# Routing stage of a two-layer encoder kernel: the last tile's rows of x are stored from ACT's DMA queue instead of SP's

## The chip, the cores and the metric

The kernel runs on one core of one Trainium2 chip. The metric is the device time of the whole program in microseconds (us), the median of several executions. The profile shown below is of one execution of the same kernel.

## What is computed

Two layers work on x, 512 rows of 1024 values in float32. Each layer has a token mixer of three parts (latent attention, a matrix LSTM and a state-space scan), an output projection, a layer norm, and then a mixture of 16 experts of which every row uses two. The part of the reference around the change is this:

```
heads = jnp.concatenate([y_a, y_b, y_c], -1)
mix = jnp.einsum('bsc,cd->bsd', heads, w_out[l])
x = _layernorm(DEEPNORM_ALPHA * x + mix, ln1_g[l], ln1_b[l])
ffn = _hier_moe(x, router_group_w[l], router_group_b[l], router_expert_w[l], router_expert_b[l],
                expert_w_gate[l], expert_w_up[l], expert_w_down[l])
x = _layernorm(DEEPNORM_ALPHA * x + ffn, ln2_g[l], ln2_b[l])
...
# _hier_moe: the best of 4 groups, the best 2 of its 4 experts, weights from two softmaxes
h = jax.nn.silu(jnp.einsum('bsd,edf->bsef', x, w_gate)) * jnp.einsum('bsd,edf->bsef', x, w_up)
h = h * combine[..., None]
return jnp.einsum('bsef,efd->bsd', h, w_down)
```

## The kernel before

The 512 rows are four tiles of 128. A layer runs through the mixer, then the routing stage (output projection, first layer norm and choice of experts), then the experts one after another, then a last stage that adds up and norms. The change is in the routing stage, which each of the two layers runs once; "layer 0" and "layer 1" name the two passes.

**Routing.** Class Tile_ holds one tile's steps and the string WSEQ their order. For a tile, f finishes the first layer norm: the left half is done by ACT and POOL or, for the last tile, all of it by DVE in two pieces (L1824 to L1826), and then a DMA of 512 KB stores the tile's 128 rows into x1d, a buffer in DRAM (L1827). keep then stores the same rows into acc, where the experts' results are added later (L1831). Both stores of all tiles are issued by SP, which also issues the loads of all weights (L277). SP's instructions stand in one queue, in order.

**Experts.** An expert handles a block of 96 rows. Expert 0's rows are picked with one-hot matmuls straight from SBUF (xz). For every other expert, index forms the row numbers on PE (matmuls of tokr with the one-hot tile ohs) and on DVE (slr, slx), and gather lets POOL issue an indirect DMA that fetches the rows from x1d (L1451). The gather of expert 1 therefore waits until all four tiles' stores into x1d have landed. Behind it POOL sets a mark (L1836), and the loads that SP issues from there on are held until the mark. When the rows of expert 1 are there, x turns them on PE (eight transposes against ident into two PSUM banks, b_74 and b_73), ACT copies the high parts (xt<-b_74, xt<-b_73) and DVE forms the low parts under the same names. up(0) is the first multiplication by the expert's weights.

**Weights of the experts.** expert_weights computes, from the logits, the weight of each row and expert on DVE and ACT, and stores it as three bf16 parts in tokw: CAST tokw, subtract (wt<-wt,tokw), CAST tokw, subtract, CAST tokw. weights then has PE multiply tokw by the one-hot tiles of experts 0, 1 and 2. On PE these twelve small matmuls stand behind the transposes of expert 1 and ahead of its up(0).

**What sets the order.** The routing and the expert stage are written once; a scheduler orders each engine's instructions from the dependencies and its own estimates of time, except for those pinned with keep_in_program_order. Each engine then runs its list in order. A change of one instruction's engine can thus move others on the same and on other engines. Tiles live in 37 reused slots; the slot of the last tile's rows z becomes free for another tile only when both its stores have been read out.

Of the kernel before, what the change touches and what calls it, by code (L numbers as in the profile page):

```python
# [20 lines left out]
NT = S // 128  # L21
# [191 lines left out]
def tile_trunk(ctx: ExitStack, tc: tile.TileContext, ins, out, dbg=None, depth=DEPTH):  # L213
    nc = tc.nc
# [7 lines left out]
    class Pinned:  # L222
# [3 lines left out]
        def __getattr__(self, k):  # L226
            f = getattr(self.e, k)

            def g(*a, **kw):
                r = f(*a, **kw)  # L230
                if pin[0] and self.n in (PINS if pin[0] is True else pin[0]):
                    tc.keep_in_program_order(r)
                return r
            return g
# [321 lines left out]
    x1d = drp.tile([S, D], F32, name="x1d")  # L556
# [4 lines left out]
    for l in range(depth):  # L561
# [820 lines left out]
        def chain(f):  # L1382
            for hd in range(HEADS):
                yield from f(hd)
# [392 lines left out]
        class Tile_:  # L1777
# [42 lines left out]
            def f(self):  # L1820
                z, n = self.z, self.ph
                if n:
                    self.cp = A.activation(z[:, 0:n], z[:, 0:n], AF.Identity, scale=self.rs)
                    G.tensor_add(z[:, 0:n], z[:, 0:n], ln1[1][:, 0:n])  # L1824
                for a, b in ((n, D),) if n else ((0, 512), (512, D)):
                    V.scalar_tensor_tensor(z[:, a:b], z[:, a:b], self.rs, ln1[1][:, a:b], op0=OP.mult, op1=OP.add)  # L1826
                self.st = nc.sync.dma_start(x1d[self.s, :], z.ap)  # L1827

            def keep(self):
                tap("x1_%d_%d" % (l, self.i), self.z.ap)  # L1830
# [435 lines left out]
```

## Time and profile before

| what | us |
|---|---|
| median of 3 runs | 1042.9 (1041.09 to 1049.63) |
| the profiled execution's own time | 1043.1 |
| its span, first to last instruction | 1041.3 |
| PE busy | 985.1 (95%) |
| DVE busy | 812.8 (78%) |
| ACT busy | 632.6 (61%) |
| POOL busy | 187.4 (18%) |
| mean granted TensorE clock | 0.985 of full speed |

Times in the rows count from the span's start. The profile's groups name a line; L230 is a helper that records almost every compute instruction, so that tiles' names tell more than lines. Names are given without buffer numbers: b is a PSUM bank, s a slot, xt a tile of split operands. SPq is SP's queue of DMA issues. In a row of the timeline the bracket tells how long the engine was idle before it and what ended that.

### The profile page before, as it was taken

Reading aid. Unit: us, or ns where it says so; the run is one execution under the profiler, and the core shown is the slowest. Engines: PE = TensorE matmul, PEld = TensorE weight load, DVE = VectorE, ACT = ScalarE, POOL = GpSimd, SP = SyncE. Lnnn points to the kernel's source line nnn. Section 1 sums busy time; section 2 is a strip of 40 time slices with the busy share of each in tenths; the row PEclk is TensorE's granted clock in tenths of the full one; section 3 lists DMA queues with packets and bytes.
Section 4 is the critical chain, followed back from the end, with each engine's and each line's share of the span. In section 5 each row is a group of like instructions: output and inputs, shape, how many; then the busy total and the mean of one; then the engine's idle time right before and its main releaser. Section 6 shows DMA issues by size and latency. Waiting matters only on the chain. (4 is left out here: it accounts for less than half of the span.)

```text
span 1041.3 us, 15398 instructions
## 1 busy us (share of the span) xinstructions
PE 985.1 (95%) x5342; PEld 733.1 (70%) x5342; DVE 812.8 (78%) x1810; ACT 632.6 (61%) x1172; POOL 187.4 (18%) x172
## 2 busy tenths in 40 slices
PE   6999999999999899999899999999999979999995
PEld 6876788666688666667598767885667866667663
DVE  8995566878549799999869956588795587999986
ACT  5565635566424588889546564466672346888874
POOL 1000002242002223223000000022320112333332
PEclk9999999999999899999999999999999998999998
DMA  8201100125837789997632111001448386999944
GB/s 313 71 23 69 61 1 1 41 65 181 296 147 272 258 289 342 337 328 233 207 143 71 41 51 41 1 1 41 142 155 325 119 303 237 319 337 326 317 123 162
DMA packets 51794, 176.76 MB, mean 170 GB/s; under 512 B 8169, under 2 KB 8681, under 8 KB 51712
## 3 DMA queue, kind: packets, MB, share of 16 engines
q1 hardware_dynamic: 45216, 160.42, 43.3%
q0 software_dynamic: 6496, 15.31, 6.2%
q8 instruction: 43, 0.70, 0.3%
q14 instruction: 39, 0.32, 0.1%
HBM read 159.61 MB, written 23.59 MB: 176 GB/s over the span
## 5 line engine op out<-in xcount | busy, mean ns | idle before, releaser
L230 PE MATMUL b<-xt,s 128*128 128x512 f32 (+3 forms) x1484 | 325.3, 366 | 11.1 <-ACT s L230 9.0
L230 PE MATMUL b<-s,s 128*128 128x512 f32 (+8 forms) x1312 | 324.1, 404 | 4.8 <-ACT s L230 2.7
L230 PEld LDWEIGHTS b<-xt,s 128*128 128x128 f32 (+2 forms) x1484 | 233.4, 183 | 77.6 <-issue 12.8
L230 DVE TENSOR_TENSOR s<-s,s 128x1024 fp32r<-128x1024 f32 (+8 forms) x252 | 226.2, 922 | 56.0 <-ACT s L230 48.8
L230 ACT ACTIVATE s<-s 128x1024 fp32r<-128x1024 f32 (+4 forms) x221 | 192.4, 904 | 98.2 <-DVE s L230 38.3
L230 PEld LDWEIGHTS b<-s,s 128*128 128x128 f32 (+3 forms) x1312 | 182.8, 171 | 85.6 <-ACT s L230 18.3
L230 ACT ACTIVATE s<-b 128x512 f32<-128x512 f32 (+8 forms) x274 | 132.0, 499 | 181.0 <-PE b L230 175.7
L230 PE MATMUL b<-s,xt 128*128 128x256 f32 (+2 forms) x944 | 205.3, 357 | 0.4 <-DVE s L230 0.4
L230 PEld LDWEIGHTS b<-s,xt 128*128 128x128 f32 (+1 forms) x944 | 147.7, 186 | 36.1 <-issue 8.7
L230 DVE TENSOR_TENSOR xt<-s,xt 128x1024 fp32r<-128x1024 f32 (+1 forms) x106 | 125.8, 1193 | 14.2 <-ACT xt L230 14.0
L230 PE MATMUL b<-ident,s 128*128 128x128 f32 (+3 forms) x736 | 107.0, 271 | 20.3 <-DMA s<-x1d,slx 13.2
L230 ACT ACTIVATE xt<-s 128x1024 fp32r<-128x1024 f32 (+1 forms) x107 | 110.7, 1043 | 21.6 <-PE b L230 12.5
L230 PEld LDWEIGHTS b<-ident,s 128*128 128x128 f32 (+3 forms) x736 | 81.7, 152 | 52.1 <-DMA s<-x1d,slx 15.4
L1604 POOL DMA_INDIRECT acc<-s,slx x28 | 58.9, 2102 | 166.2 <-ACT s L230 115.5
L230 DVE TENSOR_TENSOR s<-b,s 128x192 fp32r<-128x192 f32 (+3 forms) x108 | 58.1, 549 | 15.8 <-PE b L230 10.1
L1343 POOL TENSOR_SCALAR s<-s,sums 128x512 f32<-128x512 f32 x48 | 37.3, 780 | 155.0 <-DVE sums L230 126.3
L230 ACT ACTIVATE s<-b,mx 128x512 f32<-128x512 f32 x64 | 43.9, 692 | 19.0 <-DVE mx L230 12.8
L1451 POOL DMA_INDIRECT s<-x1d,slx x30 | 40.2, 1338 | 76.9 <-PE b L230 19.2
L230 DVE TENSOR_REDUCE mx<-b 128x1 f32<-128x512 f32 x64 | 43.4, 685 | 8.8 <-PE b L230 7.9
L230 PE MATMUL b<-xt 128*96 128x512 f32 x160 | 48.1, 408 | 0.0
L230 ACT ACTIVATE s<-b,slw 96x512 f32<-96x512 f32 (+1 forms) x60 | 38.9, 683 | 5.6 <-PE b L230 3.8
L230 ACT ACTIVATE s<-s,sb 128x128 f32<-128x128 f32 x64 | 25.6, 413 | 19.4 <-DVE s L230 19.1
(251 smaller groups left out, 857.7 us busy)
## 6 DMA issues: line engine op xcount, KB each, us to landing
s<-in_w_gu_dram SPq DMA_DIRECT2D x128, 512.0 KB, 8.9
s<-in_expert_w_down_dram SPq DMA_DIRECT2D x64, 512.0 KB, 9.3
s<-in_w_inp_dram SPq DMA_DIRECT2D x36, 512.0 KB, 5.0
s<-in_w_outp_dram SPq DMA_DIRECT2D x16, 512.0 KB, 4.7
x1d<-s SPq DMA_DIRECT2D x8, 512.0 KB, 3.1
acc<-s SPq DMA_DIRECT2D x8, 512.0 KB, 4.4
s<-acc SPq DMA_DIRECT2D x8, 512.0 KB, 6.5
s<-in_x_t_dram SPq DMA_DIRECT2D x4, 512.0 KB, 5.1
```

Source lines behind the costliest of these rows:

```text
L230: r = f(*a, **kw)
L1343: (V if hd in NORMV else G).tensor_scalar(P.ap, P.ap, sums, 0.0, op0=OP.mult, op1=OP.add)
L1451: self.ga = G.indirect_dma_start(out=self.xg[:BLK], out_offset=None, in_=x1d[0:128 * n, :], in_offset=bass.IndirectOffsetOnAxis(ap=ix[:BLK ...
L1604: G.indirect_dma_start(out=acc[:, :], out_offset=bass.IndirectOffsetOnAxis(ap=self.ix[:BLK, 0:1], axis=0), in_=yt[:BLK], in_offset=None, b ...
```

## The change

The transfer that stores the rows of the last tile (i equal to NT - 1, that is 3) into x1d is issued by ACT on ACT's queue. The other three tiles' stores into x1d and all stores into acc stay on SP.

```
-                self.st = nc.sync.dma_start(x1d[self.s, :], z.ap)
+                self.st = (nc.scalar if self.i == NT - 1 else nc.sync).dma_start(x1d[self.s, :], z.ap)
```

The scheduler's lists differ in three places that matter here. SP's list only loses the store: the load of s_382 that stood behind it now stands behind the load of s_381, and the store into acc follows.

On ACT, in the routing of layer 0 (layer 1 is alike), the store stands behind the copy of bank b_69, the first half of expert 0's rows. Before:

```order
288 L230 ACTIVATE ohs_2936<-ohf_2937 128x384
289 L230 ACTIVATE s_372_3117<-b_69 128x384
290 L230 ACTIVATE s_403_3270<-s_324_2775 128x1024
291 L230 ACTIVATE s_372_3117<-b_70 128x384
292 L230 ACT_TABLE_LOAD
293 L230 ACTIVATE ge_3154<-ge_3154 128x16
294 L230 ACTIVATE xt<-s_325_2777 128x1024
295 L230 ACTIVATE md_3164<-md_3164 128x4
```

The same place as a difference:

```order
 L230 ACTIVATE s_372_3117<-b_69 128x384
-L230 ACTIVATE s_403_3270<-s_324_2775 128x1024
+L1827 DMA x1d<-s_282_2529 128x1024
 L230 ACTIVATE s_372_3117<-b_70 128x384
 L230 ACT_TABLE_LOAD
 L230 ACTIVATE ge_3154<-ge_3154 128x16
+L230 ACTIVATE md_3164<-md_3164 128x4
+L230 ACTIVATE s_403_3270<-s_324_2775 128x1024
 L230 ACTIVATE xt<-s_325_2777 128x1024
-L230 ACTIVATE md_3164<-md_3164 128x4
```

The store takes the place of a copy of weights (s_403), which moves behind the two small exponentials ge and md.

On PE, in layer 0, between the transposes of expert 1 and its up(0): ohs_2936, ohs_2939 and ohs_3250 are the one-hot tiles of experts 0, 1 and 2. Before (each pair of rows stands four times):

```order
1134 L230 MATMUL b_74<-ident,s_370_3103 128x96 x4
1135 L230 MATMUL b_73<-ident,s_370_3103 128x96 x4
1136 L230 LDWEIGHTS ohs_2936
1137 L230 MATMUL b_75<-tokw,ohs_2936 96x3
...
1144 L230 LDWEIGHTS ohs_2939
1145 L230 MATMUL b_76<-tokw,ohs_2939 96x3
...
1152 L230 LDWEIGHTS ohs_3250
1153 L230 MATMUL b_74<-tokr,ohs_3250 96x2
```

In the changed kernel the four pairs with tokr, which write into bank b_74, stand directly behind the transposes, ahead of all pairs with tokw. In layer 1 PE's list is the same in both kernels, and has tokr first already.

On DVE, in layer 0, around the low parts of expert 1's rows (xt<-b_74 and xt<-b_73). Before:

```order
623 L230 CAST tokw<-wt_3172 128x64
624 L230 TENSOR_TENSOR wt_3172<-wt_3172,tokw 128x64
625 L230 TENSOR_TENSOR s_404_3271<-s_324_2775,s_403_3270 128x1024
626 L230 CAST tokw<-wt_3172 128x64
627 L230 TENSOR_TENSOR xt<-s_325_2777,xt 128x1024
628 L230 TENSOR_TENSOR xt<-b_74,xt 128x384
629 L230 TENSOR_TENSOR xt<-b_73,xt 128x384
630 L230 TENSOR_REDUCE slw_3242<-b_75 96x1
```

And now:

```order
622 L230 TENSOR_TENSOR xt<-s_325_2777,xt 128x1024
623 L230 CAST tokw<-wt_3172 128x64
624 L230 TENSOR_TENSOR xt<-b_74,xt 128x384
625 L230 TENSOR_TENSOR wt_3172<-wt_3172,tokw 128x64
626 L230 TENSOR_TENSOR xt<-b_73,xt 128x384
627 L230 CAST tokw<-wt_3172 128x64
628 L230 COPY slr_3257<-b_74 96x1
629 L230 TENSOR_TENSOR s_406_3290<-s_406_3290,b_71 96x256
630 L230 TENSOR_TENSOR wt_3172<-wt_3172,tokw 128x64
631 L230 SCALAR_TENSOR_TENSOR slx_3256<-slr_3257,b_74 96x1
632 L230 CAST tokw<-wt_3172 128x64
```

The last CAST of tokw stood ahead of the low parts and now stands behind them, behind the copy slr of expert 2's row numbers and behind the product s_406 of expert 0. s_404, whose slot held z, stands at row 617 now, ahead of all these. In layer 1 the last CAST stood behind the low parts before as well; the same product, a subtraction and slx have come between them.

## Rows read from the trace of the kernel before

**Rows 1.** Timeline of SP, layer 0: start us, duration us, queue, line, transfer
```profile
331.76 0.43 SPq L277 DMA_DIRECT2D s<-in_w_gu_dram  x1
334.16 0.33 SPq L1827 DMA_DIRECT2D x1d<-s  x1
334.54 0.43 SPq L277 DMA_DIRECT2D s<-in_w_gu_dram  x1
335.01 1.10 SPq L1831 DMA_DIRECT2D acc<-s  x1
```

**Rows 2.** DMA issues of Rows 1: KB each, last number us from issue to landing
```profile
x1d<-s SPq DMA_DIRECT2D x1, 512.0 KB, 5.8
...
s<-in_w_gu_dram SPq DMA_DIRECT2D x1, 512.0 KB, 6.7
...
acc<-s SPq DMA_DIRECT2D x1, 512.0 KB, 7.5
```

**Rows 3.** Line L1827, all eight stores into x1d: issue to landing
```profile
DMA to landing us min/median/max: 2.6/3.1/5.8
```

**Rows 4.** Layer 1: SP's timeline, then the two stores' time to landing
```profile
848.00 0.33 SPq L1827 DMA_DIRECT2D x1d<-s  x1
848.86 1.08 SPq L1831 DMA_DIRECT2D acc<-s  x1
...
x1d<-s SPq DMA_DIRECT2D x1, 512.0 KB, 4.6
...
acc<-s SPq DMA_DIRECT2D x1, 512.0 KB, 6.9
```

**Rows 5.** Timeline of POOL: the gather of expert 1, layers 0 and 1
```profile
341.06 1.19 POOL L1451 DMA_INDIRECT s<-x1d,slx  x1 [17.67 <-DVE more L230]
...
853.60 1.12 POOL L1451 DMA_INDIRECT s<-x1d,slx  x1 [16.64 <-DVE wgt L230]
```

**Rows 6.** Timeline of PE, layer 0: transposes of expert 1, and its up(0)
```profile
345.51 1.54 PE L230 MATMUL b<-ident,s 96*128 96x96 f32 x8 [4.30 <-DMA s<-x1d,slx]
...
348.49 2.85 PE L230 MATMUL b<-xt 128*96 128x512 f32 x6
```

**Rows 7.** Timeline of PE, layer 1: transposes, tokr, tokw, up(0)
```profile
859.80 1.54 PE L230 MATMUL b<-ident,s 96*128 96x96 f32 x8 [4.73 <-DMA s<-x1d,slx]
861.94 0.40 PE L230 MATMUL b<-tokr,ohs 128*96 128x2 bf16 x4 [0.60 <-DVE s L230]
862.71 1.04 PE L230 MATMUL b<-tokw,ohs 128*96 128x3 bf16 x12 [0.36 <-DVE slr L230]
863.61 2.85 PE L230 MATMUL b<-xt,s 128*96 128x512 f32 x6
```

**Rows 8.** Timeline of DVE, layer 0: z's last piece, then s_404
```profile
333.38 0.75 DVE L230 SCALAR_TENSOR_TENSOR s<-s,nr,s 128x512 f32<-128x512 f32 x1
...
342.59 1.23 DVE L230 TENSOR_TENSOR s<-s,s 128x1024 fp32r<-128x1024 f32 x1 [0.27 <-DMA acc<-s]
```

**Rows 9.** Timeline of DVE, layer 1: expert 0's product, subtraction, last CAST of tokw
```profile
857.40 0.40 DVE L230 TENSOR_TENSOR s<-s,b 96x256 f32<-96x256 f32 x1
...
861.80 0.22 DVE L230 TENSOR_TENSOR wt<-wt,tokw 128x64 f32<-128x64 f32 x1
...
862.41 0.25 DVE L230 CAST tokw<-wt 128x64 bf16<-128x64 f32 x1
862.50 0.15 DVE L230 COPY slr<-b 96x1 f32<-96x1 f32 x1
```

**Rows 10.** Timeline of ACT: copy of bank b_69, layers 0 and 1
```profile
334.60 0.49 ACT L230 ACTIVATE s<-b 128x384 fp32r<-128x384 f32 x1 [0.75 <-PE b L230]
...
848.45 0.49 ACT L230 ACTIVATE s<-b 128x384 fp32r<-128x384 f32 x1 [0.75 <-PE b L230]
```

**Rows 11.** Busy us by stretch: PE, PEld, DVE, ACT, POOL, then PEclk, DMA, GB/s
```profile
345.30:352.00 6.70, 6.26 (x33) 5.06 (x34) 2.33 (x9) 0.98 (x2) 0.97 (x1) 0.50 0.51 194
...
857.30:867.40 10.10, 6.64 (x33) 5.27 (x34) 2.99 (x14) 0.98 (x2) 0.99 (x1) 0.50 0.50 170
```

**Rows 12.** The same view: the expert stage of layers 0 and 1
```profile
345.50:497.00 151.50, 148.25 (x768) 104.51 (x768) 137.21 (x210) 125.09 (x183) 45.66 (x28) 0.98 0.89 297
...
860.00:1010.00 150.00, 146.98 (x762) 102.46 (x762) 134.89 (x207) 121.83 (x177) 51.05 (x28) 0.98 0.85 283
```

## The prediction

> **What bounds the kernel now.** I read first the busy shares of the page: PE is busy 95% of the span, so a stall of PE is what can be won or lost. Next the table of stretches for the two expert stages: PE works 148.25 of 151.50 us and 146.98 of 150.00 us there [rows 12], so a delay at the start of this stage has almost no later gap of PE in which it could vanish, and I let it pass to the end in full. Then the timeline of PE at the start of the stage: it stands idle 4.30 us in layer 0 and 4.73 us in layer 1 until the gathered rows of expert 1 arrive [rows 6, 7]. These two stalls are the place of the change. The timelines of SP and POOL and the DMA issues show what ends them. The store of the last tile's rows into x1d is issued at 334.16 and lands after 5.8 us, at 340.0 [rows 1, 2]; the gather starts at 341.06 [rows 5], and PE at 345.51. In layer 1 the store goes out at 848.00, lands 4.6 us later at 852.6 [rows 4], the gather starts at 853.60 and PE at 859.80 [rows 5, 7]. In both layers the gather starts 1.0 to 1.1 us behind that landing. The releaser that its row names (DVE) is only the nearest update in time; the gather reads x1d and must wait for the store, and the same distance in both layers says that it does. So every us by which the store lands earlier or later moves the stall's end.
>
> **What the change removes.** It takes the store out of SP's queue. SP did not hold it up at its issue: DVE finishes the rows at 333.38 + 0.75 = 334.13 [rows 8] and SP issues at 334.16. What costs there comes after the issue. A store into x1d takes 2.6 us at best [rows 3]; this one takes 5.8 and 4.6, for the loads issued before it are still running. The transfers that follow it on SP land at 334.54 + 6.7 = 341.2 and 335.01 + 7.5 = 342.5 [rows 1, 2], so the queue delivers one transfer of 512 KB each 1.25 us or so, in the order of issue.
>
> **What it adds: a later issue on ACT.** The store now stands behind ACT's copy of b_69, which ends at 334.60 + 0.49 = 335.1 in layer 0 and at 848.45 + 0.49 = 848.9 in layer 1 [rows 10]. That is 0.9 us later than SP's issue in both. ACT's issue itself I take as SP's 0.33; it lies ahead of the copy of b_70, which waits for PE anyway, and ACT has nothing on PE's path until the rows arrive. If that cover were gone it would cost its 0.33.
>
> **How long the store then takes** is not in the trace: no transfer of the kernel before is issued by ACT. Bound below: as if alone, 2.6 us, landing at 337.7 and 851.5. Bound above: the store shares the engines so that it ends with the last of the three transfers that are under way, when acc's store ends today, 342.5 and 848.86 + 6.9 = 855.8 [rows 2, 4]. I take a value between: its own queue lets it start at once, and beside each of its packets one of SP's queue is served, so it takes the lone 2.6 plus one transfer's 1.3: 3.9 us. It then lands at 339.0 in layer 0, **1.0 us earlier**, and at 852.8 in layer 1, **0.2 us later**. The value stands nearer to the lone store because that is a row of the same transfer, and the upper bound presumes that it is served last.
>
> **Trace against page.** The rows of this case show one queue in order of issue [rows 1, 2]. The Trainium skill, page "DMA: Bandwidth & Descriptors", section "Queues, rings and completion order", says that each DMA engine takes turns packet by packet between the queues that have work; by it the sum is mine. No run here shows it for ACT.
>
> **What moves on PE and DVE.** This is the part that the diff does not tell. In layer 0 PE now has the tokr matmuls right behind the transposes. They write into b_74, which DVE must first have read for the low part. Layer 1 already has that order, so its rows price it: from the first transpose to up(0) it takes 863.61 - 859.80 = 3.81 us [rows 7], against 348.49 - 345.51 = 2.98 in layer 0 [rows 6]. Layer 0 loses **0.8 us**.
>
> In both layers DVE's last CAST of tokw, for which the twelve tokw matmuls wait, now comes behind expert 0's product, a subtraction and slx. In layer 1 before, it started at 862.41 and the tokw matmuls at 862.71 [rows 7, 9], with slr beside it at 862.50. Now slr comes first, at 862.50, then the product (0.40), the subtraction (0.22) and slx (about slr's 0.15), and then the CAST: 862.50 + 0.77 = 863.2 at small overlaps, 0.8 later than 862.41. up(0) stands behind these matmuls on PE. That is **0.8 us in each layer**, 1.6 in all. Bounds: nothing, if DVE runs ahead more than I see, and 2.4 for the three terms together as taken; I see no row for more. What hid the three instructions before was the wait for the gather: the product ran at 857.40 [rows 9], within PE's stall. That cover is gone because they now stand behind the gathered rows.
>
> **A new wait.** s_404's slot held z, so it waits for both stores. Before it started at 342.59, with acc's landing [rows 8]. DVE now has it ahead of the low parts. Behind it stand 1.23 us for itself, another weight's low part of the same size, and four small ones of 0.2: done near 345.8. The low part of b_74 is wanted about when the transposes are done, 1.54 us behind their start [rows 6], at 346.0 if the rows come 1.0 us earlier. So it is just hidden. It also caps the gain: a store that lands over 1.2 us earlier in layer 0 gives nothing more unless acc's store lands earlier too.
>
> **The sum.** -1.0 (landing, layer 0) + 0.2 (landing, layer 1) + 0.8 (PE's order, layer 0) + 1.6 (DVE's order, both) = +1.6 us. The profiled execution took 1043.1 us, 0.2 above the median of the runs, so 1044.7 us.
>
> **Rivals.**
> One, faster: the store is nearly alone on its queue (2.6 us) and the moved instructions cost nothing. Gain 1.2 (capped) and 852.6 - 851.5 = 1.1: 1043.1 - 2.3 = 1040.8. For it: half of the eight stores needed no more than the median, 3.1 [rows 3]. Against it: these were issued into an idler queue, and the DVE order is in the program.
>
> Two, slower: a second queue buys nothing, since the same engines move the bytes. Place: the store's landing. If it still takes 5.8 and 4.6 us, but starts 0.9 later in each layer, the landing terms are +0.9 and +0.9 in place of -1.0 and +0.2: 1043.1 + 1.8 + 2.4 = 1047.3. At its worst it ends with acc's store, +2.5 and +3.2: 1043.1 + 5.7 + 2.4 = 1051.2. It decides from a duration of about 4.9 us in layer 0, where the later issue eats the gain. For it: DMA is the busier the nearer the store comes. Against it: the lone store's 2.6. The Trainium skill, in the same page's section "Issuing engines are not separate DMA queues", says that starting DMAs from several engines saves only the time to issue them; it speaks for this rival, and no run here has tried it.
>
> Three, the clock. The granted clock is at half (1.2 GHz) from 345.30 to 352.00 and from 857.30 to 867.40, with PE busy 6.26 and 6.64 us in these [rows 11], after the two stalls. If a shorter stall in layer 0 keeps the clock at full (2.4 GHz), half of 6.26 comes back: 1044.7 - 3.1 = 1041.6. If the added gaps keep layer 0 at half for as long as layer 1, 3.4 us more, it loses half of that: 1046.4. For it: both stalls were followed by the fall. Against the gain: a stall of 3.3 us is left.
>
> That the change does nothing is out: the store is on ACT's list and off SP's.
>
> **Chances.** The forecast 0.50 (its own range 1043 to 1046.5); rival one 0.15; rival two 0.22, of which 0.06 lies beyond 1051; rival three 0.13, most of it the gain. The range of 1040.0 to 1050.0 takes in all but the far end of rival two. About 1% is what a measurement of this kernel can tell from no change, 10.4 us. Both stalls together are 9.0 us, so a gain over 1% would need them and the half clock gone: 0.02. A loss over 1% needs rival two beyond its worst, or more waits in the expert stage: 0.05. Within 1%: 0.93.
>
> **What would show it.** In the changed profile: the issue on ACT near 335.1 and 848.9; its time to landing near 3.9, where 2.6 is rival one and 4.6 or more is rival two; the gather about 1.0 us behind the landing; PE from first transpose to up(0) near 4.6 us in both layers, with waits for DVE ahead of the tokr and tokw matmuls; the length of the half clock. The prediction is wrong if the gather does not follow the store's landing, if DVE reaches the last CAST before the rows arrive, or if later gaps of PE in the expert stage grow or shrink by more than these terms.

## The result, and the profile after

The changed kernel takes 1051.2 us (median of 9 runs), the kernel before 1043.5 in the same number of runs beside it. The ratio is 1.006, with a 95% interval of 1.0036 to 1.0083: slower by some 6 us, less than 1%. (The two medians alone are 7.7 us apart. Below, differences of time between kernels are taken from such ratios, each to the kernel before measured beside it.) The profiled execution took 1051.1 us, its span is 1049.4 us against 1041.3 before.

The issues first: the timelines of SP and ACT in layer 0 and, behind the dots, in layer 1 (start us, duration us, queue, line, transfer, count).

```profile
331.79 1.84 SPq L277 DMA_DIRECT2D s<-in_w_gu_dram  x2
334.18 0.33 SPq L1831 DMA_DIRECT2D acc<-s  x1
...
334.69 0.34 ACTq L1827 DMA_DIRECT2D x1d<-s  x1
...
850.38 0.91 SPq L277 DMA_DIRECT2D s<-in_w_gu_dram  x2
852.78 0.33 SPq L1831 DMA_DIRECT2D acc<-s  x1
...
853.29 0.33 ACTq L1827 DMA_DIRECT2D x1d<-s  x1
```

The reader is to compare the order with [rows 1]. The store was the second of four transfers there; s_382's load and acc's store came behind it. Now SP, which no longer waits for z with the load, issues both loads in one row, then acc's store, and the x1d store is the last of the four.

POOL's gather of expert 1's rows, layers 0 and 1, answers to [rows 5]:

```profile
343.24 1.19 POOL L1451 DMA_INDIRECT s<-x1d,slx  x1 [19.82 <-DMA acc<-s]
...
862.47 1.05 POOL L1451 DMA_INDIRECT s<-x1d,slx  x1 [20.45 <-DVE tokw L230]
```

It starts 2.18 us later in layer 0. Layer 1 begins late as a whole, so there I count from the end of z's rows on DVE. z's last piece before in layer 1, then now in layers 0 and 1:

```profile
847.23 0.74 DVE L230 SCALAR_TENSOR_TENSOR s<-s,nr,s 128x512 f32<-128x512 f32 x1
...
333.41 0.74 DVE L230 SCALAR_TENSOR_TENSOR s<-s,nr,s 128x512 f32<-128x512 f32 x1
...
852.01 0.74 DVE L230 SCALAR_TENSOR_TENSOR s<-s,nr,s 128x512 f32<-128x512 f32 x1
```

Layer 1: 847.97 to 853.60 before, 5.63 us; 852.75 to 862.47 now, 9.72 us, 4.1 us more. (In layer 0 the same count is 6.93 and 9.09.)

PE, from expert 1's transposes to its up(0), in layer 0 and layer 1, answers to [rows 6, 7]:

```profile
347.82 1.54 PE L230 MATMUL b<-ident,s 96*128 96x96 f32 x8 [6.60 <-DMA s<-x1d,slx]
349.89 0.41 PE L230 MATMUL b<-tokr,ohs 128*96 128x2 bf16 x4 [0.53 <-DVE xt L230]
351.45 1.05 PE L230 MATMUL b<-tokw,ohs 128*96 128x3 bf16 x12 [1.15 <-DVE tokw L230]
...
867.13 1.54 PE L230 MATMUL b<-ident,s 96*128 96x96 f32 x8 [7.28 <-DMA s<-x1d,slx]
869.27 0.41 PE L230 MATMUL b<-tokr,ohs 128*96 128x2 bf16 x4 [0.60 <-DVE s L230]
870.80 1.05 PE L230 MATMUL b<-tokw,ohs 128*96 128x3 bf16 x12 [1.12 <-DVE tokw L230]
```

up(0) starts at 352.36 and 871.71. The way from the first transpose to it is 4.54 us where it was 2.98, and 4.58 where it was 3.81.

Last, the DMA engines from 332 to 345 us: busy tenths in 40 slices of 0.325 us, then the packets, MB and share of SP's queue (q1) and ACT's (q10).

```profile
DMA  9978887995479744779989999999999752110000
...
q1 hardware_dynamic: 811, 2.93, 64.8%
q10 hardware_dynamic: 144, 0.52, 9.9%
```

q10 is the store and nothing else. Its first packet is recorded at 338.7, 4.0 us behind the issue at 334.69 (in layer 1 it is 3.6 us; the expectation of the first run below has 338.5 and 3.8). In between the engines are down to 4 or 5 tenths twice (slices 9 and 10, 14 and 15, counted from 0), so they were not full all the time that the store waited.

### The profile page after: what moved, and what is told of

Same layout as the page of the kernel before. It is cut to its first block, busy times and chain, and to the rows that moved or that the text cites. A ratio compares the mean times of both kernels' runs of the same rounds, so it can differ in the third digit from the quotient of the medians.

```text
span 1049.4 us, 15399 instructions
## 1 busy us (share of the span) xinstructions
PE 985.1 (94%) x5342; PEld 731.9 (70%) x5342; DVE 812.9 (77%) x1810; ACT 632.5 (60%) x1172; POOL 189.6 (18%) x172
## 5 line engine op out<-in xcount | busy, mean ns | idle before, releaser
L1604 POOL DMA_INDIRECT acc<-s,slx x28 | 61.2, 2185 | 163.0 <-ACT s L230 151.5
L230 ACT ACTIVATE xt<-b 128x384 fp32r<-128x384 f32 (+1 forms) x56 | 26.9, 526 | 18.6 <-PE b L230 18.3
```

The source lines that it names most:

```text
L1604: G.indirect_dma_start(out=acc[:, :], out_offset=bass.IndirectOffsetOnAxis(ap=self.ix[:BLK, 0:1], axis=0), in_=yt[:BLK], in_offset=None, b ...
```

## The experiments

Two theories of the late landing went in. A, order of issue: what SP and ACT have issued is worked off in the order of issue, whichever queue it came by, and the store lost two places. B: a transfer on ACT's queue starts late by itself. Beside them stood the prediction's claim that the order on DVE and PE is a cost of its own.

**All four tiles' x1d stores on ACT.**

```diff
-                self.st = nc.sync.dma_start(x1d[self.s, :], z.ap)
+                self.st = nc.scalar.dma_start(x1d[self.s, :], z.ap)
```

> The stores of all four tiles' rows into x1d are issued by ACT, not the last tile's alone. Two theories of why the last tile's store landed 2.2 us later in layer 0 than before. Theory A (order of issue): the DMA engines work off what SP and ACT have issued in the order of issue, whichever queue it came by; the store lost the two places that it had ahead of s_382's load and acc's store. Theory B (late start): a transfer of ACT's queue starts about 3.8 us after its issue whatever else is under way, as the first packets did in the changed kernel (issue 334.69, packets from 338.5). The first three tiles' stores have fewer transfers ahead of them. By A they start and land as the SP stores of these tiles did, 2.6 to 3.1 us after the issue; by B their first packets come 3.8 us after the issue and they land after 5 us or more. The last tile's store is as in the changed kernel by both: gather at 343.2 in layer 0. Time: 1051 (1048 to 1054) by both, as the first tiles' stores have time.

1051.3 us, ratio 1.0071 (1.0035 to 1.0107). The last tile's gather starts 8.36 us behind z in layer 0 and 8.13 in layer 1; s_381's load moves up on SP here, so one transfer fewer is issued just ahead of the store than in the changed kernel. Tile 0's two stores are issued at the same time, with nothing else under way: the timelines of ACT and SP, then the DMA engines from 312 to 318 us (slices of 0.15 us), and the packets, MB and share of the two queues from 314.5 to 316.5 us.

```profile
313.33 0.36 ACTq L1827 DMA_DIRECT2D x1d<-s  x1
...
313.33 0.33 SPq L1831 DMA_DIRECT2D acc<-s  x1
...
DMA  0000000000000089999999999999999600000000
...
q10 hardware_dynamic: 100, 0.41, 50.9%
q1 hardware_dynamic: 96, 0.39, 48.5%
```

The engines start in slice 14, at 314.1, 0.8 us behind the issue; the first packet of ACT's queue comes at 314.5. B is out: nothing on ACT's queue waits 4 us of itself. But A's 2.6 to 3.1 us was wrong as well. Both stores run side by side and end together near 316.8, 3.5 us behind the issue; one queue would have served the x1d store first. Here the Trainium skill's rule, page "DMA: Bandwidth & Descriptors", section "Queues, rings and completion order", that each engine takes turns between queues, agrees with the trace (50.9% against 48.5% in the middle of the two stores).

**Last tile's x1d and acc stores both on ACT.** On the changed kernel:

```diff
-                hold(nc.sync.dma_start(acc[self.s, :], self.z.ap))
+                hold((nc.scalar if self.i == NT - 1 else nc.sync).dma_start(acc[self.s, :], self.z.ap))
```

> The last tile's store into x1d and its store into acc are both issued by ACT, in this order. Theory A (order of issue): acc's store now comes behind the x1d store, so the x1d store gets one of its two lost places back, 1.25 us: gather in layer 0 at 342.0 (changed kernel 343.24, before 341.06), and 1.2 us sooner after the store's issue in layer 1. Theory B (ACT's queue starts late by itself): no change, gather at 343.2. Time by A 1049 to 1050, by B 1051.

1049.1 us, ratio 1.0038 (1.002 to 1.0056), in A's range. The gather starts 7.94 us behind z in layer 0, 1.15 less than in the changed kernel; in layer 1 it is 9.42, only 0.3 less, where A had 1.2. The scheduler's order differs here too: the way from the first transpose to up(0) is 4.33 and 5.45 us, where the changed kernel has 4.54 and 4.58, so that the time is not that of the place alone.

**Only acc's store on ACT, x1d on SP.** The same edit of acc's store, on the kernel before.

> The other way round: the last tile's rows go into x1d by SP, as before, and its store into acc is issued by ACT. PE's order of layer 0 is the changed kernel's (tokr behind the transposes), and DVE's last CASTs of tokw also stand behind the low parts, so this run has the order's cost without the late store. Theories A and B both have the x1d store where it was: gather at 341.1 in layer 0 and 5.6 us behind the store's issue in layer 1, and a time of before plus the order terms (0.8 for PE in layer 0 and 0.8 for DVE in each layer), 1044.5 to 1046. A third theory, that the order of PE and DVE and not the landing made the loss, has 1049 to 1051 here. acc's store lands at 342.5 by A (it keeps its place) and at about 343 by B; s_404 waits for it.

1045.8 us, ratio 1.0015 (0.999 to 1.004). Without the late store the loss is about 1.6 us, not 6; the third theory is out. But the order is not quite the changed kernel's: the way to up(0) is 4.05 and 4.04 us, 0.5 less in each layer than there. The gather starts sooner than A had it, 339.7, but its rows came 7.2 us later, where the kernel before needed 4.45.

**One load fewer ahead, on the changed kernel.**

```diff
-NU = 7
+NU = 6
```

> The changed kernel with one load fewer issued ahead of the stage (NU 6 in place of 7): s_382's load comes behind acc's store, when the gather is already issued. Theory A (order of issue): one transfer fewer ahead of the x1d store, 1.25 us: gather in layer 0 at 342.0 and 1.2 us sooner behind the issue in layer 1; time 1049 to 1050. Theory B (late start of ACT's queue): first packets still 3.8 us after the issue, gather at 343.2 or a little sooner because fewer loads share the engines; time 1050 to 1052. If the later load of s_382 makes the expert stage wait, it shows as a wait of ACT for that load 40 us later and adds to the time by both.

1048.4 us, ratio 1.0046 (1.002 to 1.0072). The gather starts 7.70 and 8.71 us behind z, 1.4 and 1.0 less than in the changed kernel: A's 1.25. q10's first packets come 2.0 and 2.1 us behind the issue where they took 4.0 and 3.6, which B forbids.

**DVE's order taken back, on the changed kernel.**

```diff
-                V.tensor_copy(tokw[:, :, :, c], wt)
+                cast = V.tensor_copy(tokw[:, :, :, c], wt)
...
-            ex[1].x()
+            with tc.issue_after(cast.ins):
+                ex[1].x()
```

(expert_weights hands cast on.) The low parts of expert 1's rows then stand behind the last CAST.

> The changed kernel, with its store on ACT, but the two low parts of expert 1's rows queued on DVE behind the last CAST of tokw, in both layers; PE's list then has tokw, tokr, tokw behind the transposes, as layer 0 of the kernel before. The landing stays late by all theories (gather 343.2 in layer 0). If the order of DVE and PE is a cost of its own, the way from the first transpose to up(0) falls from 4.54 and 4.58 us to about 3.0 in both layers and the time by 1.5 + 1.6, to 1048. If the order only fills time in which PE would wait for something else, the way shrinks by less, or the time stays at 1051.

1047.2 us, ratio 1.0034 (1.0015 to 1.0053), 2.7 us less than the changed kernel by the ratios; the two intervals overlap, so the size rests on the rows. PE in layer 0, then the stores that SP and ACT issue at 334.59 and 335.10 (last number: us from issue to landing):

```profile
349.34 1.54 PE L230 MATMUL b<-ident,s 96*128 96x96 f32 x8 [7.70 <-DMA s<-x1d,slx]
350.68 0.77 PE L230 MATMUL b<-tokw,ohs 128*96 128x3 bf16 x8
351.42 0.41 PE L230 MATMUL b<-tokr,ohs 128*96 128x2 bf16 x4
352.05 0.41 PE L230 MATMUL b<-tokw,ohs 128*96 128x3 bf16 x4 [0.23 <-DVE slw L230]
...
acc<-s SPq DMA_DIRECT2D x1, 512.0 KB, 9.2
...
x1d<-s ACTq DMA_DIRECT2D x1, 512.0 KB, 8.2
```

The waits of 0.53 and 1.15 are gone, up(0) starts at 352.32, 2.98 us behind the first transpose, and so in layer 1. The stall ahead of it stays, 7.70 us. Order and landing are two separate costs. The gather starts at 344.36, 1.08 us behind the store's landing at 343.28. acc's store, issued 0.5 us ahead of it, lands at 343.75, behind it; in layer 1 acc's lands first, at 859.65 against 860.04. So what stands ahead on SP delays the start of the store on ACT (its first packets come 3.6 and 3.8 us behind the issue), but does not have to end ahead of it.

**The same order in the kernel before.** The last diff, on the kernel before.

> The same order of DVE's instructions in the kernel before: stores on SP, the two low parts behind the last CAST of tokw. Layer 0 had this order already (2.98 us from the first transpose to up(0)); layer 1 had 3.81. If the order is a cost of its own, layer 1 falls to about 3.0 and the time by 0.8, to 0.999 of before; else no change. The gather stays where it was, 341.1 and 853.6, by all theories.

1044.2 us, ratio 1.0007 (0.9985 to 1.0028): the 0.8 us expected can't be seen in the time, though the way in layer 1 fell from 3.81 to 2.98. In its profile the rows of layer 1 took 7.7 us behind the gather's start, 1.5 more than before. That alone would hide it; whether it does so in other executions is open.

**acc's store on ACT, with the order taken back.** The diffs of the third and the fifth run, on the kernel before.

> The x1d store on SP, acc's store on ACT and the two low parts behind the last CAST. Against the run with acc's store on ACT alone (4.05 and 4.04 us from the first transpose to up(0)) the way falls to 3.0 in both layers if the order is a cost of its own: 2.1 us less, 0.9995 of before; if not, 1.0015 of before as there. Gather at 339.7 in layer 0 and rows 7.2 us behind it, as there.

1044.6 us, ratio 0.9994 (0.9973 to 1.0014), 2.2 us below the run with acc's store on ACT alone (2.1 expected). The way is 2.98 us in both layers. In layer 0 the gather starts at 341.0 and the rows come 4.5 us later, as in the kernel before: the 339.7 and 7.2 of that other run were one execution's.

**Nothing on ACT, acc's store ahead of x1d.** On the kernel before (keep leaves acc's store out for this tile):

```diff
+                if self.i == NT - 1:
+                    hold(nc.sync.dma_start(acc[self.s, :], z.ap))
                 self.st = nc.sync.dma_start(x1d[self.s, :], z.ap)
```

> Everything on SP, nothing on ACT, but for the last tile acc's store is issued ahead of the x1d store; s_382's load comes behind both. Theory A (order of issue): the x1d store loses one place, as to acc's store in the changed kernel, without a second queue: the gather starts about 1.25 us later than before, 342.3 in layer 0 and 6.9 us behind the x1d issue of before in layer 1. A theory in which a second queue as such is what cost the 2.2 us has the gather at 341.1 to 341.5 (0.4 for the later issue). Time: before + 1.25 in each layer by A, 1046; before + 0.8 otherwise.

1047.2 us, ratio 1.0032 (1.0014 to 1.0049): slower than before without any second queue, as A has it. The profile does not show it well. The gather starts 6.63 us behind z in layer 0, earlier than A's 8.2, and 7.81 in layer 1, later than A's 6.9. That execution took 1042.2, the lowest of ten, so I don't read its layer 0 against A or for it.

**The changed kernel's order of issue, all on SP.** This is the run that tells place from queue, on the kernel before:

```diff
...
             tiles[NT - 1].keep()
+            tc.add_manual_dep(tiles[NT - 1].st.ins, tiles[NT - 1].ac.ins.name,
+                              mybir.DependencyInfo(mybir.DependencyClass.NoSync, mybir.DependencyReason.DATA))
```

(ac is acc's store; the lines that name it are left out.) SP then issues the loads of s_381 and s_382, acc's store, the x1d store.

> Everything on SP, nothing on ACT, in the order of issue of the changed kernel: the loads of s_381 and s_382, acc's store, and the x1d store last of the four. Place against queue: in the changed kernel the gather starts 9.1 us behind the end of z's rows in layer 0 (343.24 - 334.13). If the lost places alone made the store late (theory A), the gather starts 8.5 to 9.2 us behind z here too, and rows and PE follow as late as there. If ACT's queue itself adds to it, the store comes sooner here: 7.0 to 8.0 us behind z. PE's list has tokw ahead of the transposes, so the way to up(0) is about 2.3 to 3.0 us; time by A 1.003 to 1.005 of before, by the other 1.000 to 1.002.

POOL's gather in both layers, then the issues of layer 0 and of layer 1 (last number: us from issue to landing):

```profile
343.44 1.30 POOL L1451 DMA_INDIRECT s<-x1d,slx  x1 [20.18 <-issue]
...
859.62 1.11 POOL L1451 DMA_INDIRECT s<-x1d,slx  x1 [20.20 <-DVE tokw L230]
...
acc<-s SPq DMA_DIRECT2D x1, 512.0 KB, 7.1
x1d<-s SPq DMA_DIRECT2D x1, 512.0 KB, 8.0
...
acc<-s SPq DMA_DIRECT2D x1, 512.0 KB, 6.9
x1d<-s SPq DMA_DIRECT2D x1, 512.0 KB, 7.8
```

z ends at 333.99 and 850.44, so the gather starts 9.45 and 9.18 us behind it, as late as with ACT (9.09, 9.72); in layer 0 that is 0.25 past the upper end of what A expected. The landing needs no second queue to be late. The time, 1046.7 us, ratio 1.0013 (0.999 to 1.0035), is lower than A's 1.003 to 1.005 and can't be told from no change. Against the run with ACT's late store and the same way of 2.98 us (1.0034) the intervals overlap widely. Whether ACT's queue has a cost of its own that these rows don't show stays open: some 2 us by the two ratios, anything from nothing to 5 within their intervals.

**Both stores on ACT, one load fewer, order taken back.** The diffs of the second, fourth and fifth run together. The store has its place of the kernel before, on ACT's queue.

> ACT issues the last tile's x1d store and acc's store, one load fewer is issued ahead (s_382's comes later), and the two low parts stand behind the last CAST. Of what is issued before the x1d store only s_381's load is still under way: the place of the kernel before, but on ACT's queue. Theory A (place alone): gather 6.9 us behind the end of z's rows or 6.4 behind the issue, as before, time 0.999 to 1.000 of before. If ACT's queue itself adds 1 us or so: gather 7.4 us or more behind the issue in both layers, time 1.001 to 1.003.

The issues of layers 0 and 1:

```profile
x1d<-s ACTq DMA_DIRECT2D x1, 512.0 KB, 4.4
acc<-s ACTq DMA_DIRECT2D x1, 512.0 KB, 4.6
...
x1d<-s ACTq DMA_DIRECT2D x1, 512.0 KB, 5.4
acc<-s ACTq DMA_DIRECT2D x1, 512.0 KB, 5.6
```

4.4 and 5.4 us to landing, against 5.8 and 4.6 on SP [rows 2, 4]; the gather is 5.5 and 6.5 us behind the issue. 1042.4 us, ratio 0.9988 (0.9964 to 1.0012). The first packets come 1.0 and 0.8 us behind the issue, where they took 2.0 to 2.8 with one place lost (three runs) and 3.6 to 4.0 with two. In its old place the store can't be told to be slower on ACT, or faster.

**The kernel before with two loads fewer ahead, order taken back.** Both stores on SP; the fifth run's diff and

```diff
-NU = 7
+NU = 5
```

> Stores on SP as in the kernel before, the low parts behind the last CAST, and two loads fewer issued ahead of the stage: s_381's and s_382's come behind acc's store and the gather. If transfers are worked off in the order of issue, the x1d store now has nothing ahead of it but the end of older loads and lands as the earlier tiles' stores, about 3 us after its issue; the gather starts near 338.5 in layer 0, 2.5 us sooner than before, and as much in layer 1. Time by this 1038 to 1040 if the later loads make no new wait in the expert stage; 1043 or more if they do (waits of ACT or DVE for s_381 and s_382 some 30 us later) or if the gather takes longer beside them by as much as it starts sooner.

1040.8 us, ratio 0.9971 (0.9943 to 0.9998): just below the kernel before, a little above the 1038 to 1040 expected. Issues of layers 0 and 1, POOL in layers 0 and 1, PE in layers 0 and 1:

```profile
x1d<-s SPq DMA_DIRECT2D x1, 512.0 KB, 2.6
...
x1d<-s SPq DMA_DIRECT2D x1, 512.0 KB, 4.3
...
338.54 1.19 POOL L1451 DMA_INDIRECT s<-x1d,slx  x1 [14.47 <-DVE s L230]
...
851.41 1.39 POOL L1451 DMA_INDIRECT s<-x1d,slx  x1 [16.09 <-DVE wgt L230]
...
343.78 0.88 PE L230 MATMUL b<-ident,s 96*128 96x96 f32 x8 [1.89 <-DMA s<-x1d,slx]
...
856.28 1.54 PE L230 MATMUL b<-ident,s 96*128 96x96 f32 x8 [3.13 <-DMA s<-x1d,slx]
```

With nothing new ahead of it the store needs 2.6 us in layer 0, the price of a lone store [rows 3], and PE's stalls fall to 1.89 and 3.13 us, from 4.30 and 4.73 [rows 6, 7]. From z's end to up(0) it takes 11.80 and 13.20 us, where it took 14.36 and 15.64. In layer 0 this is the gather, 3.2 us sooner. In layer 1 the 2.5 us expected did not come: the store needs 4.3 us and the gather starts only 0.3 us sooner behind z; the rest is rows that came 1.3 us sooner behind it and 0.8 us of order. The granted clock from 338 to 356 us is 0.91, where it was 0.81: with the shorter stall, less of this stretch is at 1.2 GHz. From up(0) to the end of the expert stages no wait of PE is over 1.1 us (before, 1.4).

**All runs together**, by the place of the x1d store in the program's order of issue, counted from s_381's load, or from the store itself where that load comes later; one execution of each kernel; gather behind z's end, us, in layer 0 and layer 1, from the timelines of DVE and POOL:

| place | queue | gather behind z | runs |
|---|---|---|---|
| 1 | SP | 3.73, 5.35 | NU 5 |
| 2 | SP | 6.93, 5.63; 5.99, 5.85; 6.80, 6.32; 6.89, 6.81 | before; acc on ACT; before with order; acc on ACT with order |
| 2 | ACT | 6.05, 6.99 | both on ACT, NU 6 |
| 3 | SP | 6.63, 7.81 | acc first |
| 3 | ACT | 7.94, 9.42; 7.70, 8.71; 8.36, 8.13 | both on ACT; changed, NU 6; all tiles on ACT |
| 4 | ACT | 9.09, 9.72; 9.80, 9.87 | changed; changed with order |
| 4 | SP | 9.45, 9.18 | all on SP, x1d last |

The means of places 1 to 4 are 4.5, 6.4, 8.1 and 9.5 us, 1.4 to 1.9 for a place. In layer 1 alone, places 1 and 2 hardly differ (5.35 against 5.63 to 6.99). Within places 2 and 4 the means of the two queues are 0.1 and 0.3 us apart. In place 3 ACT is 1.2 later, by a mean of three pairs against the one pair of the untypical execution.

And by time, as ratios to before:

| | order as scheduled | order taken back |
|---|---|---|
| x1d last, on ACT | 1.0060 | 1.0034 |
| x1d second, on SP, acc on ACT | 1.0015 | 0.9994 |

Down a column the two lost places, with the change of queue, are worth 4.5 and 4.0 thousandths, 4.7 and 4.2 us; in the first column 1.0 us of this is the longer way (4.54 and 4.58 against 4.05 and 4.04). Along a row the order is worth 2.7 and 2.2 us, which is within the noise of two such runs. The two add up as far as this can tell. On SP alone the place shows in the time of the run with acc's store first (1.0032), not in that of the run with x1d last (1.0013).

## Why the prediction was right, and where it was not

It said slower by 1.6 us and within 1%, and it was slower, within 1%. But 1051.2 lies above the stated range, by 1.2 us (1.006 times its base of 1043.1 would be 1049.4). It is what rival two gave for its worst case, 1051.2, in which the store ends with acc's store: 5.7 us of landing there, 6.3 measured, and 0.4 to 0.5 us between the two landings in the run with the order taken back. That the forecast had the sign right is owed to its order terms, +2.4; its landing terms were -0.8 in sum and pulled the other way.

**The landing: wrong.** The terms were -1.0 and +0.2 us; the gather's start moved by +2.2 and +4.1. The step that failed is "its own queue lets it start at once". Its first packet came after 4.0 and 3.6 us. The prediction read the order of issue out of [rows 1, 2] for one queue and 1.25 us for each transfer, and then let a second queue stand outside this order. The runs show that it stands in it: for the gather's start places count, and no effect of the queue was found. With the same numbers, two more transfers ahead are 2 x 1.25 = 2.5 us in each layer; layer 0 measured 2.2, and of layer 1's 4.1 the other 1.6 is not explained. The second half of the failed step is that the order on SP changes when the store leaves. The two loads and acc's store no longer have z's store between them and move up. The prediction told that SP did not hold the store up; it did not ask what the store had held up on SP.

The rule of the Trainium skill on taking turns (page "DMA: Bandwidth & Descriptors", section "Queues, rings and completion order"), by which "the sum is mine", agrees with the trace for two stores issued together; for one issued behind others the trace shows no turn for 3.6 to 4.0 us. The Trainium skill's other rule, in the same page's section "Issuing engines are not separate DMA queues", that starting DMAs from several engines saves only the time to issue them, agrees: in the same place ACT's store took 4.4 and 5.4 us, SP's 5.8 and 4.6. The Trainium skill, page "Perfetto Trace Analysis", section "DMA Instruction — HWDGE (DVE, Sync)", says that one block, locked for one instruction at a time, generates the descriptors for the sequencers that share it (it names DVE and Sync), and that an issue's time in the profile takes in the wait for this block and its use. ACT's issue lasts 0.34 us, like SP's of 0.33, so by that rule the store did not wait there. What holds it for the rest of the 4.0 us is not shown by any run here.

**The issue on ACT: off by 0.4.** Expected at 335.1, behind the copy of b_69; it came at 334.69. The copy started at 334.63, and the issue did not wait for its end.

**PE's and DVE's order: right.** +1.56 us in layer 0 where 0.8 + 0.8 was the sum, +0.77 in layer 1 where 0.8 was. The waits are on DVE ahead of tokr and tokw, as the prediction had them. Taking the order back gave 2.7 and 2.2 us of time for 3.2 and 2.1 us of these rows (in the changed kernel 0.8 of the 3.2 us is layer 1's, which the kernel before had too). s_404 waits for the stores, as said, 2.41 us of DVE, and is hidden as said.

**The shift passes to the end in full: right in sum, not on the way.** up(0) of layer 0 starts 3.87 us later. Some comes back first, some goes again: PE's waits from 346 to 480 us, then from 480 to 500, of the changed kernel (total us, times, longest).

```profile
PE b L230 <- DMA s<-x1d,slx: 7.7, 5, 6.6
...
PE b L230 <- ACT s L230: 1.3, 1, 1.3
```

The first row holds the stall of 6.6; the four other waits for gathered rows make 1.1 us. Before, five such waits behind the stall made 2.7, so 1.6 came back. Then PE waits 1.3 us for ACT, where it was 0.6, and between 500 and 520 us the granted clock is 0.83 where it was 0.91. I break this down no further. Layer 0 hands 4.78 us on to layer 1 (z's end, 852.75 against 847.97), and at up(0) of layer 1 it is 871.71 - 863.61 = 8.1: 4.78 + 4.09 for the landing - 1.54 for rows that came sooner behind the gather + 0.77 for the order. The span is 8.1 longer. The prediction had no term for the rows; they came 4.66 us behind the gather's start, not 6.20.

**The clock: rival three's loss did not come.** Stretches of the changed kernel (busy us of PE, PEld, DVE, ACT, POOL, then PEclk, DMA, GB/s), to be read against [rows 11]:

```profile
345.79:356.03 10.24, 6.52 (x33) 5.16 (x34) 3.48 (x15) 1.93 (x3) 0.97 (x1) 0.50 0.53 189
...
864.62:874.86 10.24, 6.01 (x32) 4.79 (x33) 3.02 (x13) 1.93 (x3) 0.98 (x1) 0.50 0.57 201
```

Layer 0 is at half clock, 1.2 GHz, for 3.5 us longer, as the rival had it. But the longer stretch holds the longer wait: behind up(0)'s start it lasts 352.00 - 348.49 = 3.5 us before and 356.03 - 352.36 = 3.7 now. That is no loss to speak of.

## What to carry to other kernels

When a transfer is moved to another engine's queue, write down the order in which all queues issue, before and after, and count the transfers that stand ahead of it; its queue may not matter at all, and what it leaves behind moves up. A store that something waits for can be sped up by issuing fewer loads ahead of it: here that, with the order taken back, was just faster than both kernels, 0.9971, though the gather itself came clearly sooner in layer 0 only; the choice of queue gave nothing that could be told. And where an instruction list comes out of a scheduler, price its changed order by itself; here it was 2.3 us by the rows, of the 8.1 us by which the span grew.

## What the runs showed of the hardware that was not expected

A DMA that ACT issues goes out while ACT's own copy is still running: 334.69, 0.06 us behind the start of a copy of 0.49 us. Two 512 KB stores that SP and ACT issue at the same time share the engines in nearly equal parts (100 and 96 packets from 314.5 to 316.5), start 0.8 us behind the issue and end together after 3.5. A store on ACT's queue, issued behind three transfers on SP's, waits 3.6 to 4.0 us for its first packet (two kernels, both layers), though the engines are at times half idle in this while.
